# Store of the third group's regrouped q made as four stores in the list of V's stores, in a hybrid attention and recurrence block

## The chip, the cores and the metric

The kernel runs on one core of one Trainium2 chip. The core has a matrix engine (TensorE, PE), a vector engine (VectorE, DVE), an activation engine (ScalarE, ACT), a general engine (GpSimd, POOL) and a queue engine (SyncE, SP) that issues most transfers (DMA) between the large memory and the on-chip memory. Every engine takes its own instructions in order; semaphores hold an instruction back until what it needs is done. The metric is device time in microseconds (us) for one execution; the median of several is given, and one more execution was profiled.

## The reference, cut to what matters

One decoder block for 2048 positions of width 1024. A combined projection gives q, k and v for three groups of eight heads, an attention gate, the input and gate of a linear recurrence (RG-LRU), and merge gates:

```
proj = x @ w_in + b_in                                  # 1024 -> 72 blocks of 128 columns
q, k, v, g_attn, u_lru, g_lru, gate_logits = split(proj)
q, k = rope(q), rope(k)
for g, (window, dilation) in enumerate(((128, 1), (512, 4), (2048, 16))):
    o_g, lse_g = dilated_band_attention(q[:, :, g], k[:, :, g], v[:, :, g], window, dilation)
attn = sum(softmax(lse) * o) * silu(g_attn);        y_a = attn @ w_attn_proj
h = rg_lru(causal_depthwise_conv(u_lru));           y_b = (h * silu(g_lru)) @ w_lru_proj
out = (sigmoid(gA) * y_a + sigmoid(gB) * y_b) @ w_out + b_out
x = layer_norm(alpha * x + out)
```

In the third group (dilation 16) a query sees keys at distances that are multiples of 16, so positions are regrouped by their residue modulo 16: residue r, then the position within it.

## The kernel before, in words

**Stages.** Stage A (to about 1434 us) computes the projection and, while TensorE multiplies, everything that follows from it position by position: rotary q and k, transposed v, gates, the recurrence. Results go to scratch tensors in the large memory. Stage B is attention, stage C the remaining projections, the merge and the norm.

**Stage A's products.** The sequence is cut into four chunks of 512 columns, c = 0 to 3. Pairs of output blocks are computed for two chunks at once, by a scheme that takes seven products of 512 x 512 blocks instead of eight; sums and differences of weight blocks (S1 to S4 in the code, tiles S) and of input blocks (T1 to T4, xT) go in. One product is twelve matmuls: four slices times three terms (high by high, high by low, low by high part), `product`, L616, matmuls at L634. For every unit of seven products, `load_w` (L232, issue at L234) loads weight blocks as tiles wA and wS; `added` (L242, L245) has GpSimd add a block by an accumulating transfer into wS; `add_w` (L247, through the helper at L227) makes the sums S on VectorE; `prep_w` (L264) splits a block into its high part hA or hS (ScalarE, L269) and its low part l (VectorE, L227). In the first half (chunks 0 and 1) the low parts are stored (L282, wl_scr); in the second they are read back (L287).

**The order.** The program writes each engine's instructions by hand in a loop over the 506 products (L955 on). One turn does: the product, the loads and preparations that are due (`events`), what was put off (`later`), the chains, the evacuation of the product's result, and `store_v`. A chain is a generator that treats one result block. At each `yield Ask(...)` it stops until at least `lag` products have passed, enough of the 34 slots of 128 x 512 on-chip memory are free (`need`), and the engines' planned budgets for this product allow it. `give` frees a slot; `give_sent` (L150) frees it two products after a store was issued.

**The q and k chain**, `qk_chain` (L299): four copies per block swap halves of the heads (sw, L307); VectorE multiplies by cos and sin and adds. k is stored at L330. q of the third group (blocks 8 to 11) is scaled and regrouped by ScalarE into rq (L336), sixteen residues times 32 positions; one product later its store is issued at L339, the whole 256 KB in one transfer, for each of the 16 residues a run of 32 floats per partition. There are sixteen such stores: four blocks, four chunks.

**V's stores.** `v_chain` (L353) transposes a block into vs and appends four stores (64 KB each, runs of 32 floats) to the list `v_store`. `store_v` (L368, issue at L373), called once at the end of each product, issues the first in the list, and two if more than six are in it.

**The recurrence**, `lru`, has small gate matmuls g (L495) that run in the middle of a product. Their inputs are the high part vh (ScalarE, L485) and the low part vl (VectorE, L486, shown at the helper's L227) of v, the convolution's result (L471), and the gate weights gw. The gates first take vh, then vl.

**Later readers.** Stage B loads the third group's q from qh_scr (L853).

Of the kernel before, what the change touches and what calls it, by code (L numbers as in the profile page):

```python
# [31 lines left out]
def hybrid_block_kernel(ctx: ExitStack, tc: tile.TileContext, a: dict, out: bass.AP):  # L32
    nc = tc.nc
    sp, act, dve, pool, pe = nc.sync, nc.scalar, nc.vector, nc.gpsimd, nc.tensor

    def flat(t):
        return t.bitcast(F32)
# [14 lines left out]
    qk_scr = {(n, u): dram.tile([P, S], F32, name=f"{n}_scr{u}") for u in range(12) for n in ("qh", "ql", "k")}  # L52
# [41 lines left out]
    def later(lag, fn):  # L94
        late.append((now["n"] + lag, fn))
# [37 lines left out]
    def take(name, dt=F32R):  # L133
        if not vacant:
            raise RuntimeError(f"no slot at {now['n']}: {[x[1].name if hasattr(x[1],'name') else x[1] for x in home.values()]} chains {len(chains)}")
        i = vacant[0]
        if name[0] == "y" and now["n"] >= base[NQ - 1]:
            i = next((x for x in LATE if x in vacant), i)
            if i in LATE:
                LATE.remove(i)  # L140
        vacant.remove(i)
        t = sl_p.tile([P, CH], dt, tag=f"s{i}", name=name)
        home[id(t)] = (i, t)
        return t

    def give(*ts):
        for t in ts:
            vacant.append(home.pop(id(t))[0])

    def give_sent(*ts):  # L150

        for t in ts:
            later(2, lambda t=t: give(t))
# [72 lines left out]
    def tt(eng, out, in0, in1, op):  # L226
        eng.tensor_tensor(out=out, in0=in0, in1=in1, op=op)  # L227
# [67 lines left out]
    def blocks(t, g):  # L295

        return t.rearrange("p (r j) -> p j r", r=4 if g == 1 else 16)

    def qk_chain(rw, f, c):  # L299
        isq = f < FT_K  # L300
        u = f % 12
        g = u // 4
        nm = f"{f}_{c}"
        yield Ask(need=1)
        sw = take("sw" + nm)
        for b in range(4):
            sp.dma_start(flat(sw)[32 * b:32 * b + 32], flat(rw)[32 * (b ^ 1):32 * (b ^ 1) + 32])  # L307
        cos, sin = CS[c % 2]
        if c < 2:
            yield Ask(lag=3, DVE=1.42)  # L310
            tt(dve, flat(rw), flat(rw), cos, ALU.mult)
            tt(dve, flat(sw), flat(sw), sin, ALU.mult)
            yield Ask(lag=0, need=1 if g and not (g == 2 and isq) else 0, DVE=1.25 if g and not (g == 2 and isq) else .72)
        else:
            yield Ask(lag=3, DVE=1.0, POOL=1.7)
            tt(dve, flat(rw), flat(rw), cos, ALU.mult)
            tt(pool, flat(sw), flat(sw), sin, ALU.mult)
            yield Ask(lag=1, need=1 if g and not (g == 2 and isq) else 0, DVE=1.2 if g and not (g == 2 and isq) else 1.0)
        if g == 0 or (g == 2 and isq):
            rp = rw  # L320
            tt(dve, flat(rp), flat(rw), flat(sw), ALU.add)
            give(sw)
        else:
            rp = take("rp" + nm)
            v, r = "p (j r) -> p j r", 4 if g == 1 else 16
            tt(dve, blocks(flat(rp), g), flat(rw).rearrange(v, r=r), flat(sw).rearrange(v, r=r), ALU.add)
            give(rw, sw)
        if not isq:
            yield Ask()
            sp.dma_start(qk_scr["k", u][:, c * CH:(c + 1) * CH], flat(rp))  # L330
            give_sent(rp)
            return
        if g == 2:
            yield Ask(need=1, ACT=.9)
            rq = take("rq" + nm)
            act.activation(blocks(flat(rq), g), flat(rp).rearrange("p (j r) -> p j r", r=16), AF.Copy, scale=0.125)  # L336
            give(rp)
            yield Ask()
            sp.dma_start(qk_scr["qh", u].rearrange("p (r i) -> p r i", r=16)[:, :, 32 * c:32 * c + 32],  # L339
                         flat(rq).rearrange("p (r i) -> p r i", r=16))  # L340
            give_sent(rq)
            return
        yield Ask(need=1, ACT=.66, DVE=.72 if c < 2 else .9)
        hi = take("hi" + nm)
        act.activation(hi, flat(rp), AF.Copy, scale=0.125)
        dve.scalar_tensor_tensor(out=rp, in0=flat(rp), scalar=0.125, in1=flat(hi), op0=ALU.mult, op1=ALU.subtract)
        yield Ask()
        for t, part in ((hi, "qh"), (rp, "ql")):
            sp.dma_start(qk_scr[part, u][:, c * CH:(c + 1) * CH], flat(t))
        give_sent(hi, rp)  # L350
# [15 lines left out]
    v_store = []  # L366
# [214 lines left out]
    def result(s, fi, c, bank, u):  # L581
# [10 lines left out]
        if kind in ("qk", "v"):  # L592
            y = take("y" + nm)
            total(flat(y), bank, u, f, sgn, True)
            start_chain(qk_chain(y, f, c) if kind == "qk" else v_chain(y, sgn, f, c))
        elif kind == "mg":
            y = take("y" + nm, F32)
            total(y, bank, u, f, sgn, False)
            start_chain(mg_chain(y, sgn, f, c))
        elif kind == "ga" or not fi:  # L600
            y = take("y" + nm, F32)
            total(y, bank, u, f, sgn, False)
            start_chain(silu_chain(y, sgn, f, c))
        else:
            i = f - FT_U
            if c == 1 and i in put_off:
                y = take("y" + nm, F32)
                total(y, bank, u, f, sgn, True)
                act.activation(ubs[:, i, 2, 0:3], y[:, CH - 3:CH], AF.Copy)
                start_chain(store_chain(y, u_scr[i]))  # L610
                return
            ub = ub_free.pop(0)
            total(ub[:, 3:3 + CH], bank, u, f, sgn, True)
            start_chain(lru(i, c, ub), 7 if c % 2 else 0)
# [115 lines left out]
    for s, pl in enumerate(plan):  # L730
        if pl[4] == "ug" and not (pl[0] and pl[1][1][0] - FT_U in put_off):
            at(base[s] + 1, lambda i=pl[1][1][0] - FT_U: fetch_gr(i))
        if pl[0] and pl[4] == "ug":
            i = pl[1][1][0] - FT_U
# [421 lines left out]
    for i in range(NG):  # L1156
        u = i // 4
# [233 lines left out]
    for n in range(32):  # L1391
        c, f = divmod(n, 8)
# [159 lines left out]
    for tt in range(16):  # L1552
        c, b = divmod(tt, 4)
# [68 lines left out]
```

## Time and profile before

| | |
|---|---|
| median of 3 runs | 2093.61 us (2092.12 to 2096.92) |
| profiled execution | 2094.05 us, of which the span of the profile 2092.3 us |
| TensorE busy | 2067.2 us, 99% of the span |
| VectorE, ScalarE, GpSimd busy | 1656.8, 1104.3, 472.0 us (79, 53, 23%) |
| TensorE busy in the first 1434 us | 1420.41 us |
| transfers | 516.26 MB, 247 GB/s on average; 173056 packets under 512 B |
| SyncE's queue (q1) | 349232 packets, 480.63 MB |
| transfers at L339, qh_scr<-rq | 16, 256 KB each, 5.7 us from issue to landing (median) |
| transfers at L373, v_scr<-vs | 192, 64 KB each, 3.6 us |
| transfers at L234, wA<-in_w_in | 253, 256 KB each, 4.7 us |

How to read the lines below. A line of a timeline has the start in us from the span's start, the length in us, the engine (PE, DVE, ACT, POOL; SPq is SyncE's queue of issues), the line of the code, the operation, the tiles written and read (out<-in), how many instructions were merged, and in brackets the idle time before it with what ended it. In a list of waits stand the waiting instruction, what it waited for, the total in us, the number of waits and the longest. A line of the chain of work has the start, the length, and what it is. A line of windows has the stretch, its length, the busy time and number of instructions of each engine, the granted TensorE clock (1.00 is full speed), the share of time in which transfers were under way, and GB/s. In a line for one tile stand the count, the least, median and greatest duration in ns, and the first and last start.

### The profile page before, as it was taken

How to read it: one execution, taken by the hardware profiler on the slowest of the kernel's cores; microseconds unless marked ns; L12 is line 12 of the kernel's file. 1: busy time of each engine (PE TensorE's matmuls, PEld its weight loads, DVE VectorE, ACT ScalarE, POOL GpSimd, SP SyncE). 2: the span in 40 equal slices, each digit the busy share in tenths (PEclk: the TensorE clock that was granted, in tenths of full speed). 3: DMA queues.
4: the chain of work that ended last, by engine and by line, in shares of the span. 5: the costliest groups of instructions: out<-in, count | busy, mean ns of one | idle time of the engine just before them, and what ended most of it. 6: DMA issues, size and time to landing. Idle time of an engine off the chain costs nothing.

```text
span 2092.3 us, 35071 instructions
## 1 busy us (share of the span) xinstructions
PE 2067.2 (99%) x11696; PEld 1706.9 (82%) x11696; DVE 1656.8 (79%) x3146; ACT 1104.3 (53%) x2293; POOL 472.0 (23%) x436
## 2 busy tenths in 40 slices
PE   8999999999999999999999999999999999999998
PEld 7888778888878888888887888888888888888887
DVE  8888788898888878778888887877999545576667
ACT  6447355356356566667666667667999411211100
POOL 1111111111111012232222232221425244331120
PEclk9999999999999999999999999999999999999999
DMA  9987988998988977768789879789996788964431
GB/s 273 277 247 242 240 272 238 286 267 251 254 278 242 320 234 198 243 203 239 237 259 268 276 231 275 240 225 358 332 340 196 238 302 276 302 223 158 149 106 71
DMA packets 369589, 516.26 MB, mean 247 GB/s; under 512 B 173056, under 2 KB 178176, under 8 KB 366080
## 3 DMA queue, kind: packets, MB, share of 16 engines
q1 hardware_dynamic: 349232, 480.63, 72.1%
q0 software_dynamic: 12256, 19.42, 5.6%
q10 hardware_dynamic: 7920, 13.97, 1.8%
q8 instruction: 93, 1.52, 0.3%
q14 instruction: 88, 0.72, 0.1%
HBM read 312.95 MB, written 186.25 MB: 239 GB/s over the span
## 4 chain that ended last, share of the span: by engine, by line
PE 77%; ACT 8%; DMA 1%; SPq 1%; DVE 1%; issue 0%; DVEq 0%; ACTq 0%
PE q L634 53%; ACT p L1053 7%; PE yb L1370 3%; PE yb L1371 3%; PE z L1482 3%; PE z L1481 3%; PE yb L1372 3%; PE z L1480 3%; PE ya L1450 1%; PE ya L1449 1%; PE ya L1448 1%; PE g L495 1%; ACT ptb L1077 1%; PE o L1094 1%; PE bc L1312 1%; PE pt L1064 0%
## 5 line engine op out<-in xcount | busy, mean ns | idle before, releaser
L634 PE MATMUL q<-xT,hS 128*128 128x512 f32 x1680 | 519.0, 390 | 0.0
L634 PE MATMUL q<-xT,l 128*128 128x512 f32 x1120 | 436.4, 390 | 0.0
L634 PE MATMUL q<-xB,hA 128*128 128x512 f32 x1248 | 388.6, 393 | 5.6 <-ACT xB L215 5.6
L634 PEld LDWEIGHTS q<-xT,hS 128*128 128x128 f32 x1680 | 314.3, 188 | 69.6 <-issue 5.2
L634 PE MATMUL q<-xB,l 128*128 128x512 f32 x904 | 353.2, 391 | 0.0
L634 PEld LDWEIGHTS q<-xB,hA 128*128 128x128 f32 x1248 | 235.5, 189 | 58.2 <-ACT xB L215 5.6
L634 PEld LDWEIGHTS q<-xT,l 128*128 128x128 f32 x1120 | 210.8, 188 | 44.1
L634 PEld LDWEIGHTS q<-xB,l 128*128 128x128 f32 x904 | 170.6, 189 | 35.9 <-DVE l L227 0.3
L1053 ACT ACTIVATE p<-p,sta 128x256 f32<-128x256 f32 (+1 forms) x384 | 174.5, 492 | 0.7 <-DVE sta L1045 0.4
L634 PE MATMUL q<-xT,hA 128*128 128x512 f32 x560 | 174.7, 393 | 0.0
L634 PE MATMUL q<-xB,hS 128*128 128x512 f32 x560 | 172.9, 390 | 0.0
L245 POOL DMA_DIRECT2D wS<-in_w_in_dram x70 | 61.9, 960 | 484.7 <-DMA wS<-in_w_in_dram 191.1
L269 ACT ACTIVATE hA<-wA 128x512 fp32r<-128x512 f32 x218 | 134.3, 624 | 49.7 <-DMA wA<-in_w_in_dram 16.0
L269 ACT ACTIVATE hS<-S 128x512 fp32r<-128x512 f32 x175 | 108.3, 625 | 81.8 <-DVE S L227 17.0
L227 POOL TENSOR_TENSOR S<-S,wA 128x512 f32<-128x512 f32 x35 | 50.2, 1435 | 350.8 <-DVE S L227 204.8
L634 PEld LDWEIGHTS q<-xT,hA 128*128 128x128 f32 x560 | 105.7, 190 | 24.1 <-issue 2.4
L634 PEld LDWEIGHTS q<-xB,hS 128*128 128x128 f32 x560 | 104.8, 188 | 23.0 <-issue 1.5
L1045 DVE CUSTOM_DVE_ANT_0 p<-s,mask 128x256 f32<-128x256 f32 (+1 forms) x384 | 119.1, 388 | 0.2 <-PE s L1038 0.2
L227 DVE TENSOR_TENSOR l<-wA,hA 128x512 fp32r<-128x512 f32 x113 | 78.6, 696 | 30.7 <-ACT hA L269 29.5
L1481 PE MATMUL z<-wo,mh 128*128 128x512 f32 (+1 forms) x264 | 101.0, 383 | 0.0
L1482 PE MATMUL z<-wo,ml 128*128 128x512 f32 (+1 forms) x264 | 101.0, 383 | 0.0
L1480 PE MATMUL z<-wo,mh 128*128 128x512 f32 (+1 forms) x264 | 101.0, 383 | 0.0
(204 smaller groups left out, 4183.0 us busy)
## 6 DMA issues: line engine op xcount, KB each, us to landing
wA<-in_w_in_dram SPq DMA_DIRECT2D x253, 256.0 KB, 4.7
wl_scr<-l SPq DMA_DIRECT2D x105, 512.0 KB, 5.2
l<-wl_scr SPq DMA_DIRECT2D x105, 512.0 KB, 4.5
sw<-y SPq DMA_DIRECT2D x384, 64.0 KB, 3.1
wS<-in_w_in_dram SPq DMA_DIRECT2D x70, 256.0 KB, 4.7
wS<-in_w_in_dram POOLq DMA_DIRECT2D x70, 256.0 KB, 6.2
v_scr<-vs SPq DMA_DIRECT2D x192, 64.0 KB, 3.6
B<-k_scr SPq DMA_DIRECT2D x24, 512.0 KB, 7.0
```

The lines of the kernel that those rows point to most:

```text
L227: eng.tensor_tensor(out=out, in0=in0, in1=in1, op=op)
L245: pool.dma_start(t, w_part(s, x), accum_op=ALU.add)
L269: act.activation(h, r, AF.Copy)
L634: pe.matmul(bank, w[:, ks], x[:, kk, xx], start=(first and i == 0 and not onto), stop=(last and i == 11), skip_group_check=onto)
L1045: dve.tensor_tensor_reduce(out=st["p", i, j][:, h, lo:256], in0=st["s", i, j // 2][h][:, j % 2, lo:256], in1=mask[:, lo:256], scale=1.0, s ...
L1053: act.activation(p, p, AF.Exp, scale=-1.0, bias=s[:, h:h + 1], accum_out=s[:, 2 + h:3 + h])
L1370: pe.matmul(yb, WL[f][:, 0, k], xx[:, 0], start=(k == 0), stop=False)
L1371: pe.matmul(yb, WL[f][:, 0, k], xx[:, 1], start=False, stop=False)
L1372: pe.matmul(yb, WL[f][:, 1, k], xx[:, 0], start=False, stop=(k == 7))
L1480: pe.matmul(z, mh[:, k], w[:, 0, hs], start=(k == 0), stop=False)
L1481: pe.matmul(z, mh[:, k], w[:, 1, hs], start=False, stop=False)
L1482: pe.matmul(z, ml[:, k], w[:, 0, hs], start=False, stop=(k == 7))
```

## The change

In the third group's branch of `qk_chain`, the store of rq is no longer issued by the chain. It is cut into four by residues (0 to 3, 4 to 7, 8 to 11, 12 to 15), and the four stores are appended to `v_store`, behind the stores of V that are in it; the slot of rq is freed two products after the last of the four was issued. `store_v` is not changed.

```diff
             yield Ask()
-            sp.dma_start(qk_scr["qh", u].rearrange("p (r i) -> p r i", r=16)[:, :, 32 * c:32 * c + 32],
-                         flat(rq).rearrange("p (r i) -> p r i", r=16))
-            give_sent(rq)
+            dst, src = (t.rearrange("p (r i) -> p r i", r=16) for t in (qk_scr["qh", u], flat(rq)))
+            for r in range(0, 16, 4):
+                v_store.append((dst[:, r:r + 4, 32 * c:32 * c + 32], src[:, r:r + 4], rq if r == 12 else None))
             return
```

## The prediction

> **What bounds the kernel now.** The change touches the projection stage, the first 1434 us, in which TensorE runs one product after another. So the first view to read is TensorE's list of waits: in that stage a microsecond counts only if TensorE waits for it.
>
> ```profile
> PE g L495 <- DVE vl L227: 8.0, 2, 5.3
> PE q L634 <- ACT xB L215: 5.6, 1, 5.6
> ```
>
> Two waits of the gate matmuls for vl (8.0 us) and one at the start of the kernel, which the change cannot reach. Now the timeline of TensorE at those two places, and behind them the chain of work at a third place, near 422 us, with the same code and no wait.
>
> ```profile
> 258.35 0.50 PE L495 MATMUL g<-vh,gw 64*128 64x512 f32 x2
> 264.14 0.80 PE L495 MATMUL g<-vl,gw 64*128 64x512 f32 x2 [5.29 <-DVE vl L227]
> ...
> 272.01 0.62 PE L634 MATMUL q<-xT,hS 128*128 128x512 f32 x2
> ```
>
> ```profile
> 578.26 0.50 PE L495 MATMUL g<-vh,gw 64*128 64x512 f32 x2
> 581.48 0.80 PE L495 MATMUL g<-vl,gw 64*128 64x512 f32 x2 [2.72 <-DVE vl L227]
> ...
> 585.05 0.62 PE L634 MATMUL q<-xB,hA 128*128 128x512 f32 x2
> ```
>
> ```profile
> 422.66 0.89 PE g L495 x5
> 423.55 62.78 PE q L634 x276
> ```
>
> The undisturbed place sets the pace: a set of gate matmuls takes 0.89 us, and one matmul of a product 62.78 / 276 = 0.2275 us (2.73 us for a product of twelve). At the first place 18 matmuls of products lie between the gates and 272.01, so 13.66 us were spent on 0.89 + 18 x 0.2275 = 4.98 us of work: 8.68 us lost. At the second, six lie between: 6.79 us for 2.25 us of work, 4.53 us lost. Together **13.2 us**, while the waits themselves are only 5.29 + 2.72 = 8.0. The windows of the timeline show the rest, in the PEclk column, the third from the end:
>
> ```profile
> 264.00:266.00 2.00, 1.86 (x6) 1.11 (x7) 2.00 (x5) 0.25 (x1) 0.00 (x0) 0.50 0.96 331
> 582.00:584.00 2.00, 2.00 (x7) 1.16 (x4) 2.00 (x5) 0.14 (x1) 0.00 (x0) 0.50 0.96 292
> ```
>
> After each wait the granted clock was 0.50: the wait is paid for again in slow matmuls, 8.68 - 5.29 = 3.4 us and 4.53 - 2.72 = 1.8 us. The Trainium skill ("TensorE: Matmul & The Clock Gate", Part 1: The HAM clock gate) has the array fall to half clock after at least one idle window of about 3.4 us. By that rule the second wait is too short to do so, and the sum would be 1.8 us less; the row with 0.50 says otherwise, and the measurement decides.
>
> Why is vl late? VectorE takes its work in order, and ahead of vl stands a weight sum S that waits for a load, wA:
>
> ```profile
> 257.27 0.68 DVE L227 TENSOR_TENSOR y<-q,u 128x512 f32<-128x512 f32 x1
> 262.19 0.69 DVE L227 TENSOR_TENSOR S<-S,wA 128x512 f32<-128x512 f32 x1 [4.23 <-DMA wA<-in_w_in_dram]
> ```
>
> ```profile
> 576.75 0.69 DVE L227 TENSOR_TENSOR S<-wS,wA 128x512 f32<-128x512 f32 x1 [4.75 <-DMA wS<-in_w_in_dram]
> 577.36 0.28 DVE L227 TENSOR_TENSOR gw<-gr,gw 128x128 fp32r<-128x128 f32 x1
> 577.56 0.68 DVE L227 TENSOR_TENSOR y<-q,u 128x512 f32<-128x512 f32 x1
> 579.52 0.69 DVE L227 TENSOR_TENSOR S<-S,wA 128x512 f32<-128x512 f32 x1 [1.28 <-DMA wA<-in_w_in_dram]
> ```
>
> And why does the load come late? SyncE's queue, at both places:
>
> ```profile
> 221.00 2.42 SPq L307 DMA_DIRECT2D sw<-y  x4
> ...
> 239.90 0.58 SPq L339 DMA_DIRECT2D qh_scr<-rq  x1
> 240.57 4.77 SPq L307 DMA_DIRECT2D sw<-y  x4
> ...
> 251.77 2.15 SPq L339 DMA_DIRECT2D qh_scr<-rq  x1
> 253.96 4.74 SPq L373 DMA_DIRECT2D v_scr<-vs  x1
> 258.81 0.43 SPq L234 DMA_DIRECT2D wA<-in_w_in_dram  x1
> ```
>
> ```profile
> 557.90 0.58 SPq L339 DMA_DIRECT2D qh_scr<-rq  x1
> 558.57 4.29 SPq L307 DMA_DIRECT2D sw<-y  x4
> ...
> 569.55 0.58 SPq L339 DMA_DIRECT2D qh_scr<-rq  x1
> 570.17 4.51 SPq L373 DMA_DIRECT2D v_scr<-vs  x1
> 574.79 0.63 SPq L234 DMA_DIRECT2D wA<-in_w_in_dram  x1
> ```
>
> L339 is the store that the change splits: 256 KB in 128 x 16 = 2048 runs of 32 floats. Its own issue is short; the issue behind it takes long (4.77, 4.74, 4.29, 4.51 us), and the load of wA stands behind that.
>
> **The change part by part.** *Removed*: 16 issues at L339, each with the stall behind it. *Added*: 64 issues of a quarter (512 runs, 64 KB each, the size and run length of one of V's stores), at store_v's place, the end of a product. What such an issue costs in a crowded queue is shown by four of V's in a row:
>
> ```profile
> 108.48 4.07 SPq L373 DMA_DIRECT2D v_scr<-vs  x4
> ```
>
> So up to 1.02 us each; 0.6 (2.42 / 4, four 64-KB copies of L307) where less is under way. The sum over the kernel, 48 more issues, 29 to 49 us of SyncE's queue, is spread over 1200 us, and the bytes and runs are the same. What matters is what stands ahead of wA at the two places.
>
> *First place.* Four of V's stores are left in the list at 239.90. The list then holds eight, so that product sends two (it sends two while more than six are there), and the next two products one each: V's are out. The second lot joins with four left: two quarters go ahead of wA, the rest behind it. Between 251.77 and 258.81 (7.04 us) only two quarters remain, 1.2 to 2.0 us: 5.0 to 5.8 us saved. Before that, L339 with its stall (0.67 + 4.77 - 2.42 = 3.0 us) is replaced by one V store sent a product earlier (1.0): 2.0 saved. Together wA may be issued 7.0 to 7.8 us earlier; it has to be 262.19 - 257.88 = 4.3 us earlier to leave the path, since S can start at 257.88, behind y (one VectorE operation per 0.61 us, as from 257.27).
>
> *Second place.* Seven of V's are left at 557.90. Three products send two of V's each, two issues more than now, and the product of the second lot sends the last V and one quarter. Between 569.55 and 574.79 (5.24 us) remain 1.2 to 2.0 us: 3.2 to 4.0 saved; before that 0.67 + 4.29 - 2.42 = 2.5 saved and 2.0 spent. wA comes 3.7 to 4.5 us earlier, and needs 579.52 - 578.17 = 1.35.
>
> So wA leaves the path at both. What is late next? TensorE resumed 1.95 us after that S started, at both places. With S right behind y at its present time, that is 259.83 and 580.12; vl was wanted at 264.14 - 5.29 = 258.85 and 581.48 - 2.72 = 578.76. Waits of 0.98 and 1.36 us are left if y and what stands ahead of it stay where they are. At the second place S<-wS, ahead of y, itself waited 4.75 us for a copy whose base load stood behind the first big store and its stall, so it moves up too, by up to 2.5 us. Hence 0 to 2.3 us left together; I take 0.6, near the lower end, because the undisturbed place has vl ready before it is wanted (gates at 422.66), by 2.0 us:
>
> ```profile
> 420.01 0.69 DVE L227 TENSOR_TENSOR vl<-v,vh 128x512 fp32r<-128x512 f32 x1
> ```
>
> Whether a wait of about 1 us halves the clock isn't shown; by the second place's 1.8 us the bound is 0 to 3.6, and I take 0.
>
> *Moved*: the slot of rq. Now it is free two products after one store, then two products after the last quarter, so three to six products later (8 to 16 us); V's slots at the first lot are freed a little earlier. This costs nothing while the 34 slots suffice. If they don't, a recurrence chain starts a product later. No row shows it; the bound is one gate wait as now, 8.7 us, on either side, since a later chain could also miss a crowded moment. I take 0. *Readers of qh_scr*:
>
> ```profile
> L339 SPq DMA_DIRECT2D qh_scr<-rq x16: 576/582/2147, 80.3 to 1290.0; - x16
> L853 SPq DMA_DIRECT2D A<-qh_scr x12: 319/424/1254, 1420.3 to 1582.1; - x12
> ```
>
> The last store moves from 1290 to at most eight products later, 1312; the first load is at 1420. Nothing.
>
> **Sum**: 13.2 - 0.6 = 12.6 us. The profiled execution took 2094.05 us (span 2092.3): 2081.45. It lies 0.44 above the median of the runs, 2093.61, so the median forecast is **2081.0 us**.
>
> **Rivals.** *One place only* (or both with a rest and half a clock): 13.2 less 4.5 or 8.7 stays, so a gain of 8.7 or 4.5: 2084.9 to 2089.1. For it: the second place has a second late input, S<-wS. Against: its base load also stood behind the first big store.
>
> *The stall is not that store's, and nothing goes.* Then the queue is simply full of small runs, and quarters stall like the whole. The third place speaks for a part of this:
>
> ```profile
> 409.70 0.58 SPq L339 DMA_DIRECT2D qh_scr<-rq  x1
> 410.38 3.87 SPq L234 DMA_DIRECT2D wA<-in_w_in_dram  x1
> ```
>
> There the store is whole, the issue behind it takes 3.87 us, and TensorE does not wait: what is lacking there is V's list. If V's stores were the cause alone, wA would move by no more than the rows leave, and a wait like the second stays at each place or turns up at a later set of gates: gain within 4.2 us either way, 2089.4 to 2097.8. Against it: fewer runs stand ahead of wA in any case, 1024 instead of 2560 at the first place. The Trainium skill ("DMA: Bandwidth & Descriptors", Rules for kernel authors) speaks against the change here too: many small transfers should be coalesced, for small ones are mostly overhead. The row of four V stores, 4.07 us, bears out an overhead in the queue, but one spread over four products is not one in a row.
>
> *Slower.* The quarters that go out behind the second lot, one per product, stand among the loads of the next unit. Each may push these by 0.6 to 1.0 us, and with them the next unit's sums. It decides once vl comes more than the 2.0 us of the undisturbed place later: three quarters ahead of one load. The price is a wait like the first, 8.7 us at each place. With the old waits only moved and one such wait new, 2093.6 + 8.7 = 2102.3. Against it: a load is asked for products ahead of its use, and SyncE has 2.73 us per product for one such store.
>
> **How the numbers follow.** Forecast 0.62 (2080.4 to 2082.7 by the rests of 0 to 2.3); one place 0.14; nothing 0.15; slower 0.09. The range goes from the fastest run shown less the whole loss, 2092.12 - 13.2 = 2078.9, to 2090.5, which takes in the forecast, the one-place case and a small part of the third. About 0.2%, 4.2 us, is what a measurement of this kernel can tell from no change. Faster by more: 0.62 + 0.13 (4.5 us is near the edge) = 0.75; within: 0.16; slower: 0.09.
>
> **What would show it.** Right: no long issue behind a store of qh_scr; wA near 258.8 issued at least 4 us earlier against the gates; TensorE's waits for vl under 2 us in total; no window at 0.50 after the start. Wrong: stalls of over 3 us behind quarters; the same 8.0 us of waits for vl at these or other gates; waits of TensorE for l or xB in the second half.

## The result, and the profile after

The changed kernel takes **2086.7 us** (median of 7 runs, 2083.95 to 2089.91) against 2093.61 us before (7 runs, 2091.03 to 2096.92): 0.9964 of the time, 95% interval 0.9951 to 0.9976. The gain of 6.9 us lies in the stated range and has the stated sign, but is little more than half of the 12.6 us that were forecast. The profiled execution took 2088.65 us, its span 2086.9.

TensorE's list of waits after the change (waiting instruction, what it waited for, us in total, times, longest):

```profile
PE q L634 <- ACT xB L215: 5.5, 1, 5.5
PE g L495 <- DVE vl L227: 2.4, 3, 1.4
PE q L634 <- DVE l L227: 1.1, 1, 1.1
```

The waits for vl fell from 8.0 to 2.4 us, and a new one for a low part l is there. SyncE's queue and TensorE at the first place (start, length, instruction):

```profile
238.28 2.80 SPq L307 DMA_DIRECT2D sw<-y  x4
...
247.62 1.51 SPq L373 DMA_DIRECT2D qh_scr<-rq  x2
249.23 0.91 SPq L234 DMA_DIRECT2D wA<-in_w_in_dram  x1
```

```profile
258.15 0.50 PE L495 MATMUL g<-vh,gw 64*128 64x512 f32 x2
258.57 0.50 PE L495 MATMUL g<-vl,gw 64*128 64x512 f32 x2
```

Two quarters stand ahead of the load, as counted out, and cost 1.6 us together. The four copies of the heads' halves take 2.80 us instead of 4.77, since no big store is ahead of them. The load of wA is issued 8.9 us before the gates; before the change it was issued 0.5 us after they began. The second set of gate matmuls follows the first at once. One window of the timeline (PEclk is the third column from the end) shows that the clock stays up as well:

```profile
260.00:270.00 10.00, 10.00 (x45) 8.26 (x44) 7.21 (x13) 8.88 (x14) 1.74 (x2) 1.00 1.05 331
```

So the first place is cured, wait and clock. The second is not quite: SyncE, VectorE and TensorE there.

```profile
566.89 1.72 SPq L373 DMA_DIRECT2D qh_scr<-rq  x1
568.71 1.46 SPq L234 DMA_DIRECT2D wA<-in_w_in_dram  x1
```

```profile
571.66 0.69 DVE L227 TENSOR_TENSOR S<-wS,wA 128x512 f32<-128x512 f32 x1 [3.35 <-DMA wS<-in_w_in_dram]
...
572.47 0.68 DVE L227 TENSOR_TENSOR y<-q,u 128x512 f32<-128x512 f32 x1
574.90 0.69 DVE L227 TENSOR_TENSOR S<-S,wA 128x512 f32<-128x512 f32 x1 [1.75 <-DMA wA<-in_w_in_dram]
```

```profile
574.99 0.50 PE L495 MATMUL g<-vh,gw 64*128 64x512 f32 x2
576.85 0.50 PE L495 MATMUL g<-vl,gw 64*128 64x512 f32 x2 [1.36 <-DVE vl L227]
```

The load is 2.8 us earlier against the gates than before (6.28 us ahead of them instead of 3.47), not 3.7 to 4.5, and it takes 6.2 us from issue to its use instead of 4.7. VectorE has been done with y, the operation ahead of S, for 1.75 us when wA arrives: the load that was to leave the path is still the last input here. A wait of 1.36 us is left. And at a place that had no wait before, TensorE now stands still:

```profile
317.84 0.61 PE L634 MATMUL q<-xB,hA 128*128 128x512 f32 x2
...
319.52 0.50 PE L634 MATMUL q<-xB,l 128*128 128x512 f32 x1 [1.07 <-DVE l L227]
...
321.68 0.77 PE L495 MATMUL g<-vl,gw 64*128 64x512 f32 x2 [0.31 <-DVE vl L227]
...
325.37 0.62 PE L634 MATMUL q<-xT,hS 128*128 128x512 f32 x2
```

Between 317.84 and 325.37 lie twelve matmuls of products and a set of gates: 7.53 us for 0.89 + 12 x 0.2275 = 3.62 us of work. 3.9 us are lost, of which the waits (1.07, 0.31 and one of 0.15 for vh) are 1.5. Most of the rest is again a halved clock: 3.4 us at 0.50, which cost 1.7.

```profile
322.00:324.00 2.00, 2.00 (x7) 1.16 (x6) 2.00 (x4) 0.85 (x2) 0.85 (x2) 0.50 0.90 297
```

The first scores of stage B tell what is left in the end: 1433.92 us before, 1428.65 after. From there on the two executions run alike.

```profile
1433.92 1.67 PE L1038 MATMUL s<-B,A 64*128 64x128 f32 x24
```

```profile
1428.65 1.67 PE L1038 MATMUL s<-B,A 64*128 64x128 f32 x24
```

5.3 of the 13.2 us in this execution. Two questions follow: is it really the short runs in the queue that held the load up, and where did the rest go?

### The profile page after: what moved, and what is told of

It is laid out like the page before. It is cut to its first block, busy times and chain, and to the rows that moved or that the text cites. A ratio compares the mean times of both kernels' runs of the same rounds, so it can differ in the third digit from the quotient of the medians.

```text
span 2086.9 us, 35149 instructions
## 1 busy us (share of the span) xinstructions
PE 2066.7 (99%) x11696; PEld 1704.5 (82%) x11696; DVE 1657.9 (79%) x3146; ACT 1101.7 (53%) x2293; POOL 471.6 (23%) x436
## 4 chain that ended last, share of the span: by engine, by line
PE 66%; ACT 5%; DVE 1%; DMA 0%; issue 0%; DVEq 0%; ACTq 0%
PE q L634 39%; ACT p L1053 4%; PE yb L1370 3%; PE yb L1371 3%; PE z L1480 3%; PE z L1482 3%; PE yb L1372 3%; PE z L1481 3%; PE o L1094 2%; PE s L1038 2%; PE ya L1448 1%; PE ya L1450 1%; PE ya L1449 1%; PE pt L1064 1%; PE g L495 1%; PE bc L1312 1%
## 5 line engine op out<-in xcount | busy, mean ns | idle before, releaser
L1370 PE MATMUL yb<-h,wl 128*128 128x512 f32 x256 | 100.3, 392 | 0.0
```

Source lines behind the costliest of these rows:

```text
L1370: pe.matmul(yb, WL[f][:, 0, k], xx[:, 0], start=(k == 0), stop=False)
```

## The experiments

**The changed kernel on another chip**, beside the next three.

> The changed kernel itself, on the same chip as the next three. Every theory: about 2086.7 us, 6 to 8 us under the kernel before, with a spread of some 3 us either way. If new waits at the later gates (at 319, 483 and 577 us of its first profile) are systematic, they stand in this profile again, with 2 to 4 us in total; if they were accidents of that one execution, they are gone and the time is nearer to 2081.

Measured: 2085.85 us (2082.18 to 2086.65), ratio 0.9965 (0.9952 to 0.9977). Its profile has waits for vl of 1.7 us in all (0.31 near 320, 0.23 near 417, 1.18 near 574), a little less than the 2 to 4 expected, and no halved clock after the start; its first scores come at 1424.70, 9.2 us earlier than before the change. So small waits near 319 and 575 are there again; the one at 483 is not.

**Four quarters at the old place**, one behind the other, the list left alone:

```diff
             for r in range(0, 16, 4):
-                v_store.append((dst[:, r:r + 4, 32 * c:32 * c + 32], src[:, r:r + 4], rq if r == 12 else None))
+                sp.dma_start(dst[:, r:r + 4, 32 * c:32 * c + 32], src[:, r:r + 4])
+            give_sent(rq)
```

> Four quarters, but issued one behind the other at the old place, not through the list. Theory 1 (what counts is how many short runs stand in the queue ahead of the weight load): as before, 2091 to 2096 us, and the first place (gates at 264 us) keeps a wait of 4 to 6 us. Rival (the stall belongs to the one transfer, whose pattern is 2048 runs in one dimension; a quarter is 128 partitions by 4 runs): as the changed kernel, 2084 to 2089 us.

Measured: 2092.53 us (2090.40 to 2096.75), ratio 1.0004 (0.9995 to 1.0013): as before. Its queue, and TensorE at the first place:

```profile
252.48 4.79 SPq L341 DMA_DIRECT2D qh_scr<-rq  x4
257.32 1.05 SPq L374 DMA_DIRECT2D v_scr<-vs  x1
258.46 1.46 SPq L234 DMA_DIRECT2D wA<-in_w_in_dram  x1
```

```profile
264.74 0.80 PE L496 MATMUL g<-vl,gw 64*128 64x512 f32 x2 [5.51 <-DVE vl L227]
```

The stall has only moved from the issue behind the store into the four quarters themselves: 4.79 us, and the load is issued at 258.46. Splitting alone does nothing.

**The whole store as one entry of the list**:

```diff
-            for r in range(0, 16, 4):
-                v_store.append((dst[:, r:r + 4, 32 * c:32 * c + 32], src[:, r:r + 4], rq if r == 12 else None))
+            v_store.append((dst[:, :, 32 * c:32 * c + 32], src, rq))
```

> One whole store, but as one entry of V's list. Theory 1: V's stores go first, so at the first place the whole store comes behind the weight load and the wait of 5.3 us there goes; its stall of 4 to 5 us then falls on the loads behind it. 2084 to 2091 us. If the quarters matter by themselves (one big store stalls wherever it stands): 2091 to 2096 us, with waits for vl of 4 us or more.

Measured: 2091.88 us (2088.41 to 2093.49), ratio 0.9996 (0.9987 to 1.0005): no difference that can be told, past the upper end of the range given for theory 1 and inside that of its rival. But the waits for vl of 4 us that the rival asked for aren't in its profile: the two old ones are gone, and others are there:

```profile
248.19 1.56 SPq L234 DMA_DIRECT2D wA<-in_w_in_dram  x1
...
252.35 1.24 SPq L372 DMA_DIRECT2D qh_scr<-rq  x1
253.63 3.64 SPq L282 DMA_DIRECT2D wl_scr<-l  x1
```

```profile
321.02 0.50 PE L633 MATMUL q<-xB,l 128*128 128x512 f32 x1 [2.11 <-DVE l L227]
...
1090.85 0.50 PE L633 MATMUL q<-xB,l 128*128 128x512 f32 x1 [0.69 <-DMA l<-wl_scr]
```

The big store now goes behind wA, and its stall of 3.64 us hits what is behind it there. Moving alone gains nothing that can be told. (This profile is of its fastest run, 2088.41; what the longer ones lost besides is not shown.)

**Halves in the list** (one edit: steps of eight residues).

```diff
-            for r in range(0, 16, 4):
-                v_store.append((dst[:, r:r + 4, 32 * c:32 * c + 32], src[:, r:r + 4], rq if r == 12 else None))
+            for r in range(0, 16, 8):
+                v_store.append((dst[:, r:r + 8, 32 * c:32 * c + 32], src[:, r:r + 8], rq if r == 8 else None))
```

> Two halves in V's list instead of four quarters. Theory 1 (runs in the queue ahead of a load, at most as many at a time as a product can take): between the whole in the list (2091.9) and the quarters (2085.9), 2086 to 2090 us, with issues of 1.5 to 3 us behind a half. If any splitting will do: as the changed kernel.

Measured: 2089.99 us (2086.39 to 2092.05), ratio 0.9987 (0.9978 to 0.9996); the changed kernel on the same chip has 0.9970 (0.9959 to 0.9980). By the median it lies between the whole and the quarters, as expected, but its interval overlaps both of theirs, so the order of the three is not shown by the times alone. In its profile the first place is without a wait; the issues behind the halves there took 1.55 and 1.39 us, and two halves one behind the other 3.37. Waits of 1.87 us near 321, 1.08 near 576 and 0.85 near 641 are left, and one of 1.06 near 1092.

**The same bytes in long runs**, at the old place, in one transfer. The regrouping in memory is left out:

```diff
-            sp.dma_start(qk_scr["qh", u].rearrange("p (r i) -> p r i", r=16)[:, :, 32 * c:32 * c + 32],
-                         flat(rq).rearrange("p (r i) -> p r i", r=16))
+            sp.dma_start(qk_scr["qh", u][:, c * CH:(c + 1) * CH], flat(rq))
```

> The kernel before with the store at its old place and whole, but written in the order in which it lies on the chip: the same 256 KB in runs of 2 KB, so the regrouping in memory is left out and the third group's attention is computed on wrongly ordered q. Theory 1 (short runs): no long issue behind this store, no wait at the first place; as fast as the changed kernel or up to 3 us faster, 2083 to 2088 us. If the bytes of the transfer are what stalls the queue: 2091 to 2096 us.

Measured: 2086.64 us (2082.77 to 2087.68), ratio 0.9963 (0.9951 to 0.9975): as the changed kernel. Its queue:

```profile
248.76 0.38 SPq L339 DMA_DIRECT2D qh_scr<-rq  x1
249.19 1.09 SPq L372 DMA_DIRECT2D v_scr<-vs  x1
250.37 1.01 SPq L234 DMA_DIRECT2D wA<-in_w_in_dram  x1
```

The issue behind the store takes 1.09 us instead of 4.74, and the load follows at once. So it is not the 256 KB: it is the 2048 short runs, all in the queue at one time.

The expectation of no wait at the first place did not hold. S took the load, though issued early, only 8.3 us after its issue, and 1.55 us of waiting are left, with 3.4 us of half clock behind them; one window of it:

```profile
260.62 0.50 PE L494 MATMUL g<-vl,gw 64*128 64x512 f32 x2 [1.55 <-DVE vl L227]
```

```profile
262.00:264.00 2.00, 2.00 (x7) 1.58 (x6) 2.00 (x4) 0.97 (x2) 0.00 (x0) 0.51 0.65 242
```

From there to stage B this profile has no wait of TensorE of 0.15 us or more, not at the second place either:

```profile
564.03 1.16 SPq L234 DMA_DIRECT2D wA<-in_w_in_dram  x1
```

```profile
573.32 0.50 PE L494 MATMUL g<-vh,gw 64*128 64x512 f32 x2
573.66 0.41 PE L494 MATMUL g<-vl,gw 64*128 64x512 f32 x2
```

The load of wA is issued 9.3 us ahead of the gates there, against 6.3 in the changed kernel, although TensorE comes 1.7 us earlier than in that one. So the wait that the changed kernel keeps at the second place belongs to its quarter stores; whether their short runs or their number and place make it is not separated.

**TensorE held back after the first place**: twelve matmuls of one product repeated three times, 36 x 0.2275 = 8.2 us, two products after the gates.

```diff
         h, l = U[s, n]
+        for _ in range(PAD.get(now["n"], 0)):
+            assert first and not onto
+            for kk in range(4):
+                ks = slice(kk * P, (kk + 1) * P)
+                for w, xx in ((h, 0), (h, 1), (l, 0)):
+                    pe.matmul(bank, w[:, ks], x[:, kk, xx], start=True, stop=True)
...
+    PAD = {92: 3}
```

> The changed kernel with 36 matmuls repeated (one product's twelve, three times, 8.2 us of TensorE) two products after the first place's gates, so between 258 and 319 us. Theory A (what was won at the first place is partly given back at later gates, because TensorE now comes there before the loads and sums): the waits at 319 and 483 us of the changed kernel and the one at 577 go, and the time grows by clearly less than 8.2 us, to 2088 to 2091 us, still 2 to 5 us under the kernel before. Theory B (the later waits come of the quarter stores or of chance and have nothing to do with TensorE being early): the whole 8.2 us is added, 2093 to 2096 us.

Measured: 2091.46 us (2090.08 to 2095.08), ratio 1.0001 (0.9992 to 1.0009). Against the changed kernel that is 0.0036 more, 7.5 us of the 8.2 (6.1 by the medians against each one's kernel before). That is nearer to theory B. Its waits:

```profile
488.37 0.50 PE L495 MATMUL g<-vl,gw 64*128 64x512 f32 x2 [0.76 <-DVE vl L227]
```

```profile
582.00 0.50 PE L495 MATMUL g<-vl,gw 64*128 64x512 f32 x2 [1.35 <-DVE vl L227]
```

Of the three, only the wait near 319 went (one of 0.52 us at the first place and one of 0.66 near 1117, for a low part read back, are there instead). The others are as long as they were at 483 and 577 (0.76 and 1.36): they move along with TensorE, so they do not come of its being early. My theory A falls for all but the one near 319. For the one near 577, theory B's quarter stores have a part in it, as the run with long runs shows.

**The accumulating load earlier.** Near 319, 483 and 577 VectorE stood for 1.8, 2.6 and 3.4 us at the sum that reads wS, the block into which GpSimd's transfer adds. Near 319 it then works almost without a gap until vl, so wS sets the end there:

```profile
314.54 0.69 DVE L227 TENSOR_TENSOR S<-wS,wA 128x512 f32<-128x512 f32 x1 [1.82 <-DMA wS<-in_w_in_dram]
```

Near 577 the wait for wA (1.75) comes after it. Here the base loads of S1 and S3 and the adds go out one product earlier, in the first half only:

```diff
-            for d, n in ((6, "S1"), (6, "S3"), (4, "A11"), (3, "A12"), (d22, "A22")):
+            for d, n in ((7, "S1"), (7, "S3"), (4, "A11"), (3, "A12"), (d22, "A22")):
...
-                at(max(t0 - 4, 2), lambda s=s, n=n, x=x: added(s, n, x))
+                at(max(t0 - 5, 2), lambda s=s, n=n, x=x: added(s, n, x))
```

> The changed kernel, and in the first half the base loads of S1 and S3 and the accumulating loads on them each one product earlier. Theory A with the accumulating load as the late input (at all three later waits VectorE stood at the sum that reads wS): the waits at 319, 483 and 577 us go, 2079 to 2083 us. If the transfers as a whole are too slow there, or the late input is another: 2084 to 2088 us.

Measured: 2082.13 us (2081.35 to 2082.39), ratio 0.9954 (0.9941 to 0.9967), as by theory A. Of the waits one of 0.30 us near 320 is left. Because this and the changed kernel had been on different chips, both once more on one:

> The changed kernel once more, as the measure for the next two on one chip. 2084 to 2088 us, and a spread of 4 us or more between its executions, since its small waits differ from one to the next and some of them halve the clock.

> The changed kernel with the loads and adds of S1 and S3 one product earlier, once more. If the accumulating load is what makes the later waits: 2 to 6 us under the changed kernel on the same chip, no wait of TensorE over 0.5 us between 60 and 1430 us, and a spread under 2 us. If its first result was luck: no difference from the changed kernel.

Measured: the changed kernel 2086.23 us (2083.49 to 2089.64), ratio 0.9970 (0.9959 to 0.9980); with the earlier loads **2081.18 us** (2080.84 to 2082.23), ratio 0.9943 (0.9930 to 0.9955). The intervals don't meet: this version beats both. SyncE, VectorE and TensorE at the second place, with the earlier loads:

```profile
563.77 0.48 SPq L234 DMA_DIRECT2D wA<-in_w_in_dram  x1
```

```profile
564.74 0.69 DVE L227 TENSOR_TENSOR S<-wS,wA 128x512 f32<-128x512 f32 x1 [1.18 <-issue]
567.32 0.69 DVE L227 TENSOR_TENSOR S<-S,wA 128x512 f32<-128x512 f32 x1 [1.09 <-DMA wA<-in_w_in_dram]
568.53 0.69 DVE L227 TENSOR_TENSOR vl<-v,vh 128x512 fp32r<-128x512 f32 x1
```

```profile
570.05 0.50 PE L495 MATMUL g<-vh,gw 64*128 64x512 f32 x2
570.38 0.40 PE L495 MATMUL g<-vl,gw 64*128 64x512 f32 x2
```

VectorE no longer waits for wS, and vl is there (569.22) before the gates begin. But the last input ahead of vl is still wA (1.09), so an earlier wS alone would not have done it. The load of wA is issued 6.28 us ahead of the gates, exactly as in the changed kernel; S takes it 3.55 us after its issue (3.70 in the first run of this version) instead of 6.19. The edit moves nothing but the loads of wS, so it is their place that made wA quicker; by what way is not shown. How the start of the vl gates (last row: the first scores) moved against the kernel before, in us, by the profiles:

| place | before | changed | changed, again | with earlier loads, again |
|---|---|---|---|---|
| first place | 264.14 | 258.57 | 259.13 | 258.98 |
| second set after it | 337.49 | 332.62 | 330.76 | 329.28 |
| last before the second place | 495.88 | 492.61 | 490.01 | 487.66 |
| first after it | 646.71 | 640.94 | 638.44 | 634.06 |
| stage B | 1433.92 | 1428.65 | 1425.92 | 1421.25 |
| gain at the end | | 5.3 | 8.0 | 12.7 |

The changed kernel loses along the way part of what it has won; with the earlier loads next to nothing is lost, and 12.7 of the 13.2 us come out.

**The kernel before with the earlier loads**, its big store left as it was:

> The kernel before, with only that shift of the loads and adds by one product. The big store stays, and at the first place the wait was for a load that this doesn't move (wA): a wait of 3 to 6 us stays there, the one at 581 us gets shorter or goes: 2087 to 2093 us. If the accumulating load was the cause of the first place too: 2080 to 2086 us, and the change of the store would be worth little beside it.

Measured: 2085.31 us (2083.99 to 2094.12), ratio 0.9977 (0.9966 to 0.9988), in two groups, 2083.99 to 2085.98 (8 runs) and 2090.05 to 2094.12 (4). The expectation for the first place was wrong:

```profile
259.42 0.50 PE L495 MATMUL g<-vl,gw 64*128 64x512 f32 x2 [0.75 <-DVE vl L227]
...
576.16 0.80 PE L495 MATMUL g<-vl,gw 64*128 64x512 f32 x2 [3.21 <-DVE vl L227]
```

A wait of 0.75 us is left there, not 3 to 6. The two loads of wS are gone from between the two big stores, the issue behind the second of these takes 3.40 us instead of 4.74, and the load of wA is issued at 253.95 instead of 258.81. The second place keeps 3.21 us in this execution, one of the group of four. The median lies in the range of the second expectation: in 8 of the 12 runs the earlier loads alone bring about as much as the change does. Both together bring most, and bring it in every run.

## Why the prediction was right, and where its size was off

*The number.* 2086.7 us lies in the band that the prediction gave to its rival of one place, or both with a rest and half a clock (2084.9 to 2089.1, chance 0.14), not in that of the forecast (2080.4 to 2082.7, chance 0.62). The range held because it took in that rival. Of the four signs of being right, two came: no long issue behind a quarter at the two places, and wA earlier by 9.4 us at the first. Two did not quite: the waits for vl were 2.4, 1.7 and 2.6 us in the three profiles instead of under 2, and one of the three has a window at 0.50.

*The loss.* 13.2 us at two places, waits plus a halved clock: right. With both causes taken away, 12.4 and 12.7 us come out at the start of stage B (1421.53 and 1421.25).

*The cause.* That the big store's runs held up the load of wA: shown, by the long runs (no stall ahead of that load, and the changed kernel's time) against four quarters at once (the same stall, and the old time). The rival that the queue is full anyway, so that quarters stall like the whole, holds only where they go out together. The Trainium skill's advice to coalesce many small transfers into one large one ("DMA: Bandwidth & Descriptors", Rules for kernel authors) gives under 64 KB as the size where overhead rules, and a quarter is just 64 KB; followed here, it would have been wrong: with one transfer of 256 KB in short runs the kernel took 6.9 us more than with four of 64 KB spread over the products.

*What stands ahead of wA.* The counts were right at both places. At the first, the saving was larger than worked out (9.4 us against the gates, for 7.0 to 7.8); at the second smaller (2.8 for 3.7 to 4.5), since one quarter and the load itself took 1.72 and 1.46 us to issue and the load landed later.

*The rest, taken as 0.6 us: this is the term that was mis-sized.* The three profiles of the changed kernel miss 7.9, 4.0 and 5.2 us of the 13.2; waits of 0.15 us or more and the slow clock make up 5.6, 2.5 and 2.7 of these, and what the remainder is stays open. First, "wA leaves the path at both" failed at the second place: in all three profiles VectorE still waited for wA there (1.75, 1.28 and 1.59 us), which came 6.2 to 6.5 us after its issue instead of 4.7, and TensorE kept a wait of 1.36, 1.18 and 1.76 us. That the first of these equals the 1.36 worked out is chance, for that figure was for a wA in time. The undisturbed place near 422 us, with its 2.0 us of margin, was a poor neighbour to go by: there wS was in time. Second, "what is late next?" was asked at the two places only, not at the gates after them. Near 319 us TensorE arrives earlier by all that it won at the first place (8.7 us), and VectorE, which waits for wS and then has work almost without a gap, by 3.2 only (314.54 for 317.78). That wait goes when TensorE is held back; the others don't. With the loads and adds of wS a product earlier all of them go but 0.30 us. At the second place the wait is also gone with one store in long runs, which lets wA out 3 us earlier against the gates; so there the quarters in the queue and the loads of wS beside wA both count.

*The clock.* That a wait of about 1 us does not halve it was right for the single waits of the changed kernel (1.36 and 1.76 us, clock 1.00), and wrong for the string near 319 us in one of three executions. In the run with long runs a single wait of 1.55 us halved it.

*Slots, readers, the second half.* Nothing was seen of them: in the three profiles of the changed kernel no wait of TensorE between 660 and 1420 us reached 0.15 us. The time of the slower rival did not come.

What stays open: why the wait near 483 us is there in some executions and not in others (the kernel before with the earlier loads has one of 0.80 us near 481), why wA lands later beside the loads of wS, and the two groups of the last experiment. The profiles show single executions.

## What to carry to other kernels

Count the runs that stand in a queue ahead of a load somebody is waiting for, not the bytes; if a transfer must be in short runs, spread it over time, and leave splitting alone unless the pieces really go out apart. When a wait is taken away, follow the engine to the next places where it meets the same producer: what was hidden by the old wait is due there, and an input that is late by little at many places deserves its own edit. Price a wait of TensorE with the slow clock that can come behind it.

## What the runs showed of the hardware that was not expected

*The length of an idle time does not tell whether the clock is halved.* Idle times of 1.07, 0.15 and 0.31 us within 3.3 us were followed by 3.4 us at 0.50 in one execution, and a single wait of 1.55 us by as much in the run with long runs, while a single wait of 1.76 us left the clock at 1.00:

```profile
574.65 0.51 PE L495 MATMUL g<-vl,gw 64*128 64x512 f32 x2 [1.76 <-DVE vl L227]
```

```profile
574.00:576.00 2.00, 1.34 (x7) 0.89 (x8) 2.00 (x4) 0.19 (x1) 0.00 (x0) 1.00 1.15 337
576.00:578.00 2.00, 2.00 (x11) 1.64 (x10) 2.00 (x4) 0.96 (x2) 0.00 (x0) 1.00 1.13 316
```

The Trainium skill ("TensorE: Matmul & The Clock Gate", Part 1: The HAM clock gate) speaks of a free-running window of about 3.4 us. That the halved stretches last 3.4 or 6.8 us here agrees. Its rule of at least one idle window does not, for 1.55 us of idle time were enough.

*The spread between executions was smallest where the waits were gone.* That the waits make it is not shown by itself. On one chip the kernel before ranged over 7.3 us (19 executions), the changed one over 6.2 (9), and the version with the earlier loads over 1.4 (5).
